# Decoder step on one core: expert rows gathered in the order they are stored and reordered by the PSUM copy, first up weights in eight halves, one combine earlier

## The chip, the cores and the metric

The kernel runs on one core of a Trainium2 chip. The metric is the device time of one execution in microseconds, as the median of several runs. The profile is of one execution; its span goes from the first to the last instruction.

## The reference

One layer of a decoder for 256 prompt tokens and 8 single-token sequences with 1024 cached positions each, D = 1024, everything float32:

```python
xn = rmsnorm(x, g_mix)
q, k, v, b_gate, c_gate, h_in = jnp.split(xn @ w_in, SPLIT_POINTS, axis=-1)
att = moba_attend(rope(q), k_all, v_all, pos)          # 8 heads of 64
conv_y = b_gate * short_conv(c_gate * h_in)            # 512 channels, 3 taps
hres = x + jnp.concatenate([att, conv_y], -1) @ w_out
hn = rmsnorm(hres, g_ffn)
# two-level router: one of 4 groups, then 2 of its 8 experts; gates sum over both
h = jax.nn.silu(hn @ w_gate[e]) * (hn @ w_up[e]) * gate[e]   # 32 experts, D -> 256
y = rmsnorm(hres + sum_e h @ w_down[e], g_final)
```

The expert weights are 32 times 1 MB each of gate, up and down, 96 MB in all. They and the 33.5 MB of the paged cache are most of what the core reads.

## The kernel before

**Stages.** The first stage (to about 203 us of the profile) projects, gathers cache pages by indirect DMA, attends, convolves, applies `w_out` and routes. It is cut into some 250 named steps (`steps["H10"]` and so on); the string `ORDER` (line 36) sets in which order they are recorded, and each engine executes its instructions in that order. The second stage is a loop over eight groups of four experts (line 1273).

**Tokens** stand in three tiles: tile 0 and 1 are the prompt, 128 rows each, tile 2 holds the 8 samples (`NR`). The residual rows are `yres[token, tile, 1024]`. A token's slot within an expert is its rank among the expert's tokens, 32 slots an expert; `rank` (`prk`) counts, `onehot` (`Pg`) turns ranks into a 0/1 matrix tokens x 128 slots for the group.

**One group.** `gather_mm` multiplies `Pg` with the rows (`px`, 128 slots x 512 columns, two halves `hf` of D); `gather_rows` copies `px` from PSUM to the row tile `xr`; `gather_T` transposes it (`pxt`) and scales it into `xg`; `mm_exp` multiplies with gate (`pgt`) and up weights (`pup`), four experts side by side in 32-column strips; SiLU times up gives `sh`, its transpose `hT`; `down` gives `pyy`; `gated` scales it by the routing weight into `Y` as a high and a low part; `combine_all` spreads `Y` back to tokens (`pz`) and adds it to `yres`. The combine of a group is recorded inside the next one, behind its gate product.

**Orders of columns.** The expert weights lie in memory so that partition p holds rows 8p to 8p + 7 of D: `w_gate.rearrange("o e (p c) f -> (o e) p (c f)", c=8)`. So `xg` needs, for each c, the elements D = 8p + c. For group 0 `gather_mm` reads `yres` as f32 with that order in the moving operand:

```python
rhs=yres[:, t, :].rearrange("t (p c) -> t c p", c=8)[:, 4 * hf:4 * hf + 4, :]
```

For the later groups the rows are split once into a high and a low part (`hn`, `hlo`; `norm2_hi` a cast on ACT, `norm2_lo` a difference on DVE), and these are stored in the order (c p), so that the products read neighbours. Tile 0 is split by the last step of `ORDER` (`hl0`), tile 1 in group 0 around the up product, tile 2 after it. The copies of `gather_rows` are plain.

**Weights and queues.** SP issues the loads, in the order of recording. Expert weights go through a ring of 15 buffers of 1 MB (`tags`, line 1149: two of tag c9, nine rk, four rw, which earlier held activations, cache rows and projection weights). The order is gate 0, down 0, the first two gates of group 1, then the up weights of group 0, then the rest. Up 0 has no place in the ring: `room1` and `room2` reserve six tiles of 512 KB (`uh`, from the pool c4 of ten) and four of 256 KB (`uq`, pool c2). The loads into them are recorded behind all steps (lines 1133 to 1137 and 1155 to 1165). The tiles `xh`, `xr`, `xg`, `hn`, `hlo` and `Y` come from the pool c4 as well, in turn.

**The last group** (`LAST` = 7) loads up in halves and down in three pieces; between its gate and up products stand the combine of group 6, maps and gates (`ppt`, `pgs`), three products that put `yres` into PSUM (`before`, `pzl`) and 12 dummy products (`keep_warm`, `warm`).

Of the kernel before, what the change touches and what calls it, by code (L numbers as in the profile page):

```python
# [19 lines left out]
D = 1024  # L20
# [21 lines left out]
cv2 b3 B10 b2 V3 cv0 V0 c2 c3 ov V2 V1 B13 eB1 G25 o010 kvs pe0 o000 eB3 G26 eB0 G27 G28 G29 o110 G30 V5 eB2 V4  # L42
o001 V6 H00 G31 o011 V7 H01 l00 pa pe o100 R0 l01 L0 ra0 rb0 rc0 o101 as co room1 rd0 re0 z0 z1 rk0 oh0 y0
y1 H10 H20 H21 l20 R2 l21 L2 ra2 rb2 room2 o111 rc2 rd2 l10 o112 H11 R1p H12a R1 H12b rk2 oh2 l11 l12 L1 ra1 rb1 rc1
g00 g01 rsa g20 rk1p rk1 oh1 g21 g10 ga0 g11 gt0 ga1 rsb gt1 rd1 sl re2 re1 hl0
"""
# [42 lines left out]
def hymba_step(ctx: ExitStack, tc: tile.TileContext, x_prompt, x_sample, cache_k, cache_v, state_conv,  # L89
# [22 lines left out]
    def c4(name, shape, dt=F32):  # L112
        return wp.tile(shape, dt, name=name, tag="c4", bufs=10)
# [11 lines left out]
    with tc.manual_schedule():  # L125
# [719 lines left out]
        def norm2_hi(t, a, w):  # L845
            n, p = NR[t], slice(a // 8, (a + w) // 8)
            if a == 0:
                hn[t] = c4(f"hn{t}", [128, 8, 128], F32R)
# [4 lines left out]
            S.copy(hn[t][:n, :, p].rearrange("t c p -> t p c"),  # L853
                   yres[:n, t, a:a + w].rearrange("t (p c) -> t p c", c=8))

# [7 lines left out]
        def norm2_lo(t, a, w):  # L863

            n, p = NR[t], slice(a // 8, (a + w) // 8)
            if t not in hlo:
                hlo[t] = c4(f"hlo{t}", [128, 8, 128], F32R)
            V.tensor_tensor(
                hlo[t][:n, :, p], yres[:n, t, a:a + w].rearrange("t (p c) -> t c p", c=8),
                hn[t][:n, :, p].bitcast(F32), op=OP.subtract)  # L870

# [155 lines left out]
        def gather_mm(grp, hf, tiles):  # L1027


            if (grp, hf) not in PX:  # L1030
                PX[grp, hf] = ps("px", "qb")
            first, last = (0, 2) if grp == 1 else (0, 1)
            for t in tiles:
                if grp == 0:
                    T.matmul(PX[grp, hf], lhsT=fl(PgS[grp], t, 128).bitcast(F32),
                             rhs=yres[:, t, :].rearrange("t (p c) -> t c p", c=8)[:, 4 * hf:4 * hf + 4, :],
                             start=t == first, stop=t == last)
                    continue
                n = 40 if t == 2 else 128
                lows = (0,) if t == 2 else (0, 1)  # L1040
                for low in lows:
                    T.matmul(PX[grp, hf], lhsT=fl(PgS[grp], t, n),  # L1042
                             rhs=(hn, hlo)[low][t][:n, 4 * hf:4 * hf + 4, :].rearrange("t c p -> t (c p)"),
                             start=t == first and low == 0, stop=t == last and low == lows[-1])

        XR = {}

        def gather_rows(grp, hf):
            if hf == 0:
                XR[grp] = c4("xr", [128, 8, 128])  # L1050
            rows_, px = XR[grp][:, 4 * hf:4 * hf + 4, :].rearrange("s c p -> s (c p)"), PX.pop((grp, hf))
            w = 256 if grp == 0 else 512
            S.copy(rows_[:, 0:w], px[:, 0:w])  # L1053
            if w < 512:
                V.tensor_copy(rows_[:, w:512], px[:, w:512])

# [63 lines left out]


        SPLIT = {}

        @step("room1")
        def _():
            for j in (0, 1, 3):
                SPLIT[0, "u", j] = [c4("uh", [128, 1024]) for _ in range(2)]

        @step("room2")
        def _():  # L1130
            SPLIT[0, "u", 2] = [c2("uq", [128, 512]) for _ in range(4)]

        def load_split(grp, nm, j, lst, view):
            ts = lst[grp, j] = SPLIT[grp, nm, j]
            w = 2048 // len(ts)
            for i, t in enumerate(ts):
                SP.dma_start(t, view[4 * grp + j][:, w * i:w * i + w])

        for name in ORDER.split():
            steps.pop(name)()  # L1140
        assert not steps, steps
# [12 lines left out]

        for grp in range(NE // 4):
            for lst, view, nm in ((gw, wg_v, "g"), (uw, wu_v, "u"), (dw, wd_v, "d")):
                for j in range(4):
                    if (grp, nm, j) == (1, "g", 2):
                        for k in (0, 1, 3, 2):
                            load_split(0, "u", k, uw, wu_v)  # L1160
                    if (grp, nm, j) in SPLIT:
                        continue
                    lst[grp, j] = ring(f"{nm}{grp}{j}", next(it))
                    if grp < LAST or nm == "g":
                        SP.dma_start(lst[grp, j], view[4 * grp + j])
        for a, b in ((0, 1024), (1024, 2048)):
# [106 lines left out]
        for grp in range(NE // 4):  # L1273
# [211 lines left out]
```

## Time and profile before

| | us |
|---|---|
| median of 3 runs (lowest to highest) | 429.58 (429.26 to 432.44) |
| profiled execution | 428.75 |
| its span | 426.7 |
| PE busy | 379.3 (89%) |
| DVE, ACT, POOL busy | 198.6, 94.0, 101.6 |
| moved by DMA | 155.05 MB, mean 363 GB/s |

The profile names groups by line, engine, operation and tile ("px<-yres,Pg" is written from those two). An f32 product leaves two records. "PEclk" is the share of TensorE's full clock that was granted. A wait "A <- B: 12.8, 1, 12.8" is total us, times, longest. SPq is SP's queue of DMA issues; a DMA row there has the time of its issue, not of its transfer.

### The profile page before, as it was taken

The numbers are of one execution on the slowest core, as the hardware profiler recorded it, in microseconds if no ns is written. First come the engines' busy times: TensorE is split into PE (matmuls) and PEld (weight loads), VectorE is DVE, ScalarE is ACT, GpSimd is POOL, SyncE is SP. The second block draws the span as 40 slices with busy tenths as digits, with TensorE's granted clock in tenths as the row PEclk, the third lists the DMA queues.
The fourth block names the chain that finished last, engine by engine and source line by source line (L and its number), as shares of the span: only waits on it lengthen the run. The fifth ranks groups of instructions, "written<-read, shape, count | busy, mean of one in ns | idle before, by whom it ended". The sixth has DMA issues, their size and how long they took to land.

```text
span 426.7 us, 6625 instructions
## 1 busy us (share of the span) xinstructions
PE 379.3 (89%) x2646; PEld 208.8 (49%) x2646; DVE 198.6 (47%) x389; ACT 94.0 (22%) x240; POOL 101.6 (24%) x99
## 2 busy tenths in 40 slices
PE   7999997999999999898999999996986987969971
PEld 6354354668775335363555455642533543524530
DVE  2257986899672014671763242430430431332045
ACT  4221314274330000311640111110020130110033
POOL 2727888978306000000200000000000000000031
PEclk9999999999999999988899899996996996997997
DMA  7999987879988999949899999999999999999903
GB/s 258 395 360 416 382 340 259 326 218 413 419 335 312 422 419 423 414 150 384 323 422 424 421 419 420 422 420 422 421 419 423 419 419 422 422 416 404 322 5 104
DMA packets 33125, 155.05 MB, mean 363 GB/s; under 512 B 3084, under 2 KB 5338, under 8 KB 18244
## 3 DMA queue, kind: packets, MB, share of 16 engines
q1 hardware_dynamic: 27472, 119.70, 70.3%
q0 software_dynamic: 5008, 33.80, 20.1%
q10 hardware_dynamic: 612, 1.11, 0.7%
q8 instruction: 22, 0.36, 0.3%
q14 instruction: 11, 0.09, 0.1%
HBM read 152.41 MB, written 2.20 MB: 362 GB/s over the span
## 4 chain that ended last, share of the span: by engine, by line
PE 58%; DMA 23%; DVE 9%; issue 4%; POOL 3%; ACT 1%; SPq 1%; DVEq 0%; ACTq 0%; POOLq 0%
DMA u<-in_w_up_dram 12%; DMA g<-in_w_gate_dram 9%; PE py L779 7%; PE pgt L1205 6%; PE pup L1205 5%; PE pyy L1219 4%; PE pz L1236 4%; PE px L1042 4%; PE pov L724 3%; PE acck L242 3%; PE accB L561 3%; DVE Sd L489 3%; PE accv L242 2%; PE accq L242 2%; DMA yres<-in_x_sample_dram 2%
## 5 line engine op out<-in xcount | busy, mean ns | idle before, releaser
L1205 PE MATMUL pgt<-g,xg 128*32 128x256 f32 x512 | 47.6, 481 | 18.0 <-DMA g<-in_w_gate_dram 17.7
L1270 DVE TENSOR_TENSOR yres<-yres,pz 128x512 f32<-128x512 f32 (+1 forms) x42 | 25.7, 672 | 53.6 <-PE pz L1236 53.6
L1176 POOL TENSOR_TENSOR PGw<-Pg,G 128x384 f32<-128x384 f32 x8 | 6.7, 843 | 171.6 <-PE pgs L1181 88.1
L1205 PEld LDWEIGHTS pgt<-g,xg 128*32 128x32 f32 x512 | 21.0, 137 | 45.7 <-DMA g<-in_w_gate_dram 24.0
L483 POOL TENSOR_TENSOR K<-K,qv 128x2048 f32<-128x2048 f32 x9 | 40.7, 4538 | 5.3 <-DMA K<-in_cache_k_dram,idx 3.1
L489 DVE TENSOR_REDUCE Sd<-K 128x32 f32<-128x2048 f32 x16 | 35.9, 2276 | 5.9 <-POOL K L483 5.9
L1219 PE MATMUL pyy<-d,hT 128*32 128x512 f32 (+1 forms) x272 | 32.1, 591 | 0.6 <-DVE hT L1318 0.6
L779 PE MATMUL py<-wo,mixT 128*128 128x512 f32 (+1 forms) x72 | 29.1, 552 | 0.0
L1205 PE MATMUL pup<-u,xg 128*32 128x256 f32 x448 | 25.6, 380 | 0.0
L1236 PE MATMUL pz<-Y,PT 128*128 128x512 f32 (+1 forms) x90 | 23.1, 405 | 0.0
L1228 DVE SCALAR_TENSOR_TENSOR Y<-pyy,gsl,Y 128x512 fp32r<-128x512 f32 (+1 forms) x17 | 12.1, 719 | 23.6 <-ACT Y L1227 23.6
L1296 DVE SCALAR_TENSOR_TENSOR sh<-pup,rsl,sh 128x256 f32<-128x256 f32 x8 | 5.4, 670 | 34.1 <-PE pup L1205 26.5
L1227 ACT ACTIVATE Y<-pyy,gsl 128x512 fp32r<-128x512 f32 (+1 forms) x17 | 11.2, 660 | 45.2 <-PE pyy L1219 45.1
L315 POOL DMA_INDIRECT V<-in_cache_v_dram,idx x16 | 15.6, 974 | 22.2 <-PE pov L724 18.2
L1053 ACT COPY xr<-px 128x512 f32<-128x512 f32 (+1 forms) x16 | 8.9, 559 | 50.7 <-PE px L1042 38.6
L779 PEld LDWEIGHTS py<-wo,mixT 128*128 128x128 f32 x72 | 13.2, 190 | 12.6 <-issue 12.1
L1042 PE MATMUL px<-hn,Pg 128*128 128x512 f32 (+1 forms) x42 | 19.2, 480 | 0.0
L315 POOL DMA_INDIRECT K<-in_cache_k_dram,idx x16 | 15.5, 971 | 14.7 <-DMA K<-in_cache_k_dram,idx 7.9
L1205 PEld LDWEIGHTS pup<-u,xg 128*32 128x32 f32 x448 | 13.8, 110 | 8.6
L1236 PEld LDWEIGHTS pz<-Y,PT 128*128 128x128 f32 (+1 forms) x90 | 13.2, 155 | 9.7 <-issue 2.9
L1219 PEld LDWEIGHTS pyy<-d,hT 128*32 128x32 f32 x272 | 8.8, 112 | 17.9 <-issue 16.0
L485 DVE TENSOR_TENSOR K<-K,qb 128x2048 f32<-128x2048 f32 x7 | 16.0, 2280 | 2.3 <-DMA K<-in_cache_k_dram,idx 2.3
(333 smaller groups left out, 607.1 us busy)
## 6 DMA issues: line engine op xcount, KB each, us to landing
g<-in_w_gate_dram SPq DMA_DIRECT2D x32, 1024.0 KB, 19.8
d<-in_w_down_dram SPq DMA_DIRECT2D x28, 1024.0 KB, 17.5
u<-in_w_up_dram SPq DMA_DIRECT2D x24, 1024.0 KB, 19.9
wo<-in_w_out_dram SPq DMA_DIRECT2D x4, 1024.0 KB, 16.9
u<-in_w_up_dram SPq DMA_DIRECT2D x8, 512.0 KB, 12.1
uh<-in_w_up_dram SPq DMA_DIRECT2D x6, 512.0 KB, 11.8
wk<-in_w_in_dram SPq DMA_DIRECT2D x2, 1024.0 KB, 14.4
wv<-in_w_in_dram SPq DMA_DIRECT2D x2, 1024.0 KB
```

The source lines that it names most:

```text
L242: T.matmul(acc, lhsT=xnT[:, cc, 128 * t:128 * t + 128], rhs=W[pn, kk][:, c, :], start=cc == 0, stop=cc == 7)
L315: P.indirect_dma_start(out=t, out_offset=None, in_=src, in_offset=bass.IndirectOffsetOnAxis(ap=idx[:, b, hh:hh + 1], axis=0))
L483: P.tensor_tensor(kslots[i], kslots[i], qv[:, None, :].to_broadcast([128, 4, 512]), op=OP.mult)
L485: V.tensor_tensor(kslots[i], kslots[i], qbs[b][:, None, :].to_broadcast([128, 4, 512]), op=OP.mult)
L489: V.tensor_reduce(Sd[:, b, 4 * hh:4 * hh + 4, :].rearrange("p i h -> p (i h)"), kslots[i].rearrange("p i (h d) -> p (i h) d", h=8), axis=A ...
L561: T.matmul(acc[:, 0:264], lhsT=W[pn, kk][:, c, 128 * m:128 * m + 128], rhs=xnT[:, cc, 0:264], start=cc == 0, stop=cc == 7)
L779: T.matmul(po[:, lo:lo + w], lhsT=mixT[:, c, 128 * t:128 * t + 128], rhs=wo[n, c // 4][:, c % 4, lo:lo + w], start=c == 0, stop=c == 7, sk ...
L1042: T.matmul(PX[grp, hf], lhsT=fl(PgS[grp], t, n), rhs=(hn, hlo)[low][t][:n, 4 * hf:4 * hf + 4, :].rearrange("t c p -> t (c p)"), start=t == ...
L1205: T.matmul(dst[32 * j:32 * j + 32, 0:256], lhsT=xg[:, c, 32 * j:32 * j + 32], rhs=w[:, 256 * k:256 * k + 256], start=c == 0, stop=c == 7, ...
L1219: T.matmul(py[32 * j:32 * j + 32, 0:w], lhsT=hT[:, c, 32 * j:32 * j + 32], rhs=dw[grp, j][:, 1024 * c + a:1024 * c + b], start=c == 0, sto ...
L1236: T.matmul(pz, lhsT=PTS[grp][:, 128 * t:128 * t + NR[t]], rhs=Y[:, i, 0:w], start=start and i == 0, stop=i == 1, skip_group_check=more)
L1270: V.tensor_tensor(yv, yv, pz[:m], op=OP.add)
```

## The change

**Rows in their own order.** `gather_mm` reads `yres`, and `hn` and `hlo`, as they stand: half hf is the columns 512 hf to 512 hf + 511, that is p from 64 hf, all c. The tiles `hn` and `hlo` become plain [128, 1024] copies. `gather_rows` now writes `xr` through a rearranged view (c is 128 elements apart), so a half fills a part of all eight c; every transpose needs both halves.

**Order of the first group.** In `ORDER`, `g20 g21` stand ahead of the rank of tile 1, and the sums `rsa` behind it; both copies `ga0 ga1` stand ahead of both transposes `gt0 gt1`. The step `hl0` is gone: tile 0 and tile 1 are split in group 0 behind the up product (`norm2_hi`) and behind the gates (`norm2_lo`).

**Up 0** is eight `uh` tiles of 512 KB from c4; `uq` and `room2` are gone. The loads are recorded inside the steps `ld0` and `room1`.

**The combine of group 6** is recorded at the end of group 6 instead of behind the gate product of group 7.

```diff
-o001 V6 H00 ... as co room1 rd0 re0 z0 z1 rk0 oh0 y0
-y1 H10 H20 H21 l20 R2 l21 L2 ra2 rb2 room2 o111 ...
-g00 g01 rsa g20 rk1p rk1 oh1 g21 g10 ga0 g11 gt0 ga1 rsb gt1 rd1 sl re2 re1 hl0
+o001 V6 H00 ... as co ld0 room1 rd0 re0 z0 z1 rk0 oh0 y0
+y1 H10 H20 H21 l20 R2 l21 L2 ra2 rb2 o111 ...
+g00 g01 g20 g21 rk1p rk1 oh1 rsa g10 ga0 g11 ga1 rsb gt0 gt1 rd1 sl re2 re1
...
-            S.copy(hn[t][:n, :, p].rearrange("t c p -> t p c"),
-                   yres[:n, t, a:a + w].rearrange("t (p c) -> t p c", c=8))
+            S.copy(hn[t][:n, a:a + w], yres[:n, t, a:a + w])
...
-            V.tensor_tensor(
-                hlo[t][:n, :, p], yres[:n, t, a:a + w].rearrange("t (p c) -> t c p", c=8),
-                hn[t][:n, :, p].bitcast(F32), op=OP.subtract)
+            V.tensor_tensor(hlo[t][:n, a:a + w], yres[:n, t, a:a + w], hn[t][:n, a:a + w].bitcast(F32), op=OP.subtract)
...
-                             rhs=yres[:, t, :].rearrange("t (p c) -> t c p", c=8)[:, 4 * hf:4 * hf + 4, :],
+                             rhs=yres[:, t, 512 * hf:512 * hf + 512],
...
-                             rhs=(hn, hlo)[low][t][:n, 4 * hf:4 * hf + 4, :].rearrange("t c p -> t (c p)"),
+                             rhs=(hn, hlo)[low][t][:n, 512 * hf:512 * hf + 512],
...
-            rows_, px = XR[grp][:, 4 * hf:4 * hf + 4, :].rearrange("s c p -> s (c p)"), PX.pop((grp, hf))
-            w = 256 if grp == 0 else 512
+            rows_ = XR[grp][:, :, 64 * hf:64 * hf + 64].rearrange("s c p -> s p c")
+            px = PX.pop((grp, hf)).rearrange("s (p c) -> s p c", c=8)
+            w = 32 if grp == 0 else 64
             S.copy(rows_[:, 0:w], px[:, 0:w])
-            if w < 512:
-                V.tensor_copy(rows_[:, w:512], px[:, w:512])
+            if w < 64:
+                V.tensor_copy(rows_[:, w:64], px[:, w:64])
...
+        @step("ld0")
+        def _():
+            load(0, "g", range(4))
+            load(0, "d", range(4))
+            load(1, "g", (0, 1))
+
+        @step("room1")
+        def _():
+
+            for j in range(4):
+                uw[0, j] = [c4("uh", [128, 1024]) for _ in range(2)]
+                for i, t in enumerate(uw[0, j]):
+                    SP.dma_start(t, wu_v[j][:, 1024 * i:1024 * i + 1024])
...
-                combine_all(grp - 1, Ys)
+                if grp < LAST:
+                    combine_all(grp - 1, Ys)
                 slot_maps(grp)
                 slot_gates(grp)
-            else:
-                norm2_hi(1, 0, 512)
-                norm2_hi(1, 512, 512)
...
             if grp == 0:
                 slot_maps(grp)
+                for t in (0, 1):
+                    for a in (0, 512):
+                        norm2_hi(t, a, 512)
...
                 slot_gates(grp)
-                norm2_lo(1, 0, 512)
-                norm2_lo(1, 512, 512)
+                for t in (0, 1):
+                    for a in (0, 512):
+                        norm2_lo(t, a, 512)
                 norm2_both(2)
...
+            if grp == LAST - 1:
+                combine_all(grp, Ys)
```

**What moves on PE ahead of the first gate product.** `px` is the gather product, `prk` the rank of tile 1, `prs` the norm factor of each slot, `pxt` the transposes. Before:

```order
191 L1035 MATMUL px<-yres,Pg 128x512 x2
192 L1066 MATMUL prs<-rsb_1112,Pg 128x1
193 L1066 MATMUL prs<-rsb_1251,Pg 128x1
194 L1035 MATMUL px<-yres,Pg 128x512
195 L1001 LDWEIGHTS onesb__72
196 L1001 MATMUL prk<-A,onesb__72 128x32
197 L1001 LDWEIGHTS onesb__72
198 L1001 MATMUL prk<-A,onesb__72 128x32
199 L1008 LDWEIGHTS trib
200 L1008 MATMUL prk<-A,trib 128x32
201 L1035 MATMUL px<-yres,Pg 128x512 x3
202 L1076 MATMUL pxt<-ident,xr 128x128 x4
```

After:

```order
191 L1031 MATMUL px<-yres,Pg 128x512 x4
192 L997 LDWEIGHTS onesb__72
193 L997 MATMUL prk<-A,onesb__72 128x32
194 L997 LDWEIGHTS onesb__72
195 L997 MATMUL prk<-A,onesb__72 128x32
196 L1004 LDWEIGHTS trib
197 L1004 MATMUL prk<-A,trib 128x32
198 L1064 MATMUL prs<-rsb_1112,Pg 128x1
199 L1064 MATMUL prs<-rsb_1281,Pg 128x1
200 L1031 MATMUL px<-yres,Pg 128x512 x2
201 L1064 MATMUL prs<-rsb_1336,Pg 128x1
202 L1074 MATMUL pxt<-ident,xr 128x128 x8
```

Four of the six `px` stand ahead of the rank instead of three, two behind it, and the eight transposes come in one row.

**What SP's loads of up 0 wait for** (DMAHW names a lane of earlier transfers, the other names an engine that read or wrote the buffer). Before:

```order
33 L1137 DMA uh<-in_w_up_dram 128x1024 [waits DVE_49,DMAHW0_49,PE_49,Activation_49]
34 L1137 DMA uh<-in_w_up_dram 128x1024 [waits DMAHW1_49,PE_49]
35 L1137 DMA uh<-in_w_up_dram 128x1024 [waits DVE_49,DMAHW2_49,PE_49,Activation_49]
36 L1137 DMA uh<-in_w_up_dram 128x1024 [waits DMAHW3_49,DVE_49,PE_49]
37 L1137 DMA uq<-in_w_up_dram 128x512 [waits DMAHW4_49]
```

After:

```order
33 L1148 DMA uh<-in_w_up_dram 128x1024 [waits DMAHW0_49]
34 L1148 DMA uh<-in_w_up_dram 128x1024 [waits DMAHW1_49,Activation_49]
35 L1148 DMA uh<-in_w_up_dram 128x1024 [waits DMAHW2_49]
36 L1148 DMA uh<-in_w_up_dram 128x1024 [waits DMAHW3_49]
37 L1148 DMA uh<-in_w_up_dram 128x1024 [waits DMAHW4_49,DVE_49]
38 L1148 DMA uh<-in_w_up_dram 128x1024 [waits DMAHW5_49,DVE_49]
39 L1134 DMA g_1430<-in_w_gate_dram 128x2048 [waits DMAHW6_49,PE_49]
```

No `uh` waits for PE any more; the engine waits that are left are for the attention's tiles (lines 521, 534, 544 and 708). The gates of group 1 wait for PE, which reads `w_out` out of the same buffers.

**PE at the end of group 6.** Before, behind the gate product of group 7:

```order
944 L1205 MATMUL pgt<-g_1586,xg 32x256
945 L1236 MATMUL pz<-Y,PT 128x512 x2
946 L1236 MATMUL pz<-Y,PT 8x512 x2
947 L1236 MATMUL pz<-Y,PT 128x512 x4
950 L1192 MATMUL ppt<-ident,Pg 128x128 x2
```

After:

```order
894 L1219 MATMUL pyy<-d_1568,hT 32x512
895 L1236 MATMUL pz<-Y,PT 128x512 x2
896 L1236 MATMUL pz<-Y,PT 8x512 x2
897 L1236 MATMUL pz<-Y,PT 128x512 x4
900 L1205 MATMUL pgt<-g_1570,xg 32x256
```

The combine `pz` stood between `pgt` and `ppt` and now stands between group 6's `pyy` and `pgt`.

More of the change, by code (lines that the diff above doesn't have):

```diff
@@ L42 @@
 cv2 b3 B10 b2 V3 cv0 V0 c2 c3 ov V2 V1 B13 eB1 G25 o010 kvs pe0 o000 eB3 G26 eB0 G27 G28 G29 o110 G30 V5 eB2 V4
[L43 to L45 removed]
+o001 V6 H00 G31 o011 V7 H01 l00 pa pe o100 R0 l01 L0 ra0 rb0 rc0 o101 as co ld0 room1 rd0 re0 z0 z1 rk0 oh0 y0
+y1 H10 H20 H21 l20 R2 l21 L2 ra2 rb2 o111 rc2 rd2 l10 o112 H11 R1p H12a R1 H12b rk2 oh2 l11 l12 L1 ra1 rb1 rc1
+g00 g01 g20 g21 rk1p rk1 oh1 rsa g10 ga0 g11 ga1 rsb gt0 gt1 rd1 sl re2 re1
 """
@@ L845, in norm2_hi @@
         def norm2_hi(t, a, w):
-            n, p = NR[t], slice(a // 8, (a + w) // 8)
+            n = NR[t]
             if a == 0:
-                hn[t] = c4(f"hn{t}", [128, 8, 128], F32R)
+                hn[t] = c4(f"hn{t}", [128, D], F32R)
                 if t == 2:
@@ L863, in norm2_lo @@
         def norm2_lo(t, a, w):
-            n, p = NR[t], slice(a // 8, (a + w) // 8)
+            n = NR[t]
             if t not in hlo:
-                hlo[t] = c4(f"hlo{t}", [128, 8, 128], F32R)
-            V.tensor_tensor(
-                hlo[t][:n, :, p], yres[:n, t, a:a + w].rearrange("t (p c) -> t c p", c=8),
-                hn[t][:n, :, p].bitcast(F32), op=OP.subtract)
+                hlo[t] = c4(f"hlo{t}", [128, D], F32R)
+            V.tensor_tensor(hlo[t][:n, a:a + w], yres[:n, t, a:a + w], hn[t][:n, a:a + w].bitcast(F32), op=OP.subtract)
         def norm2_log(t, k):
@@ L1119, in hymba_step @@
         steps["rsb"] = lambda: gather_rs(0, (1,))
[L1122 to L1141, printed above, removed]
         wg_v = w_gate.rearrange("o e (p c) f -> (o e) p (c f)", c=8)
@@ L1153, in ring, with load @@
             return c9(name, (128, 2048)) if tag == "c9" else slot(name, tag)
[L1155 to L1165, printed above, removed]
+        def load(grp, nm, js):
+            lst, view = {"g": (gw, wg_v), "u": (uw, wu_v), "d": (dw, wd_v)}[nm]
+            for j in js:
+                lst[grp, j] = ring(f"{nm}{grp}{j}", next(it))
+                SP.dma_start(lst[grp, j], view[4 * grp + j])
+        @step("ld0")
[9 more added lines that the diff above has]
+                    SP.dma_start(t, wu_v[j][:, 1024 * i:1024 * i + 1024])
+        for name in ORDER.split():
+            steps.pop(name)()
+        assert not steps, steps
+        load(1, "g", (2, 3))
+        load(1, "u", range(4))
+        load(1, "d", range(4))
+        for grp in range(2, LAST):
+            for nm in "gud":
+                load(grp, nm, range(4))
+        load(LAST, "g", range(4))
+        for j in range(4):
+            uw[LAST, j] = ring(f"u{LAST}{j}", next(it))
+        for j in range(4):
+            dw[LAST, j] = ring(f"d{LAST}{j}", next(it))
         for a, b in ((0, 1024), (1024, 2048)):
@@ L1394, in hymba_step @@
             n = NR[t]
-            hs = c4("hs", [128, 8, 128])
+            hs = c4("hs", [128, D])
             V.tensor_tensor(hs[:n], hn[t][:n].bitcast(F32), hlo[t][:n].bitcast(F32), op=OP.add)
@@ L1401, in hymba_step @@
                 for c in range(4):
-                    T.transpose(pv_[:, c, 0:n], hs[:n, 4 * hf + c, :], ident[:n, :n])
+                    T.transpose(pv_[:, c, 0:n], hs.rearrange("t (p c) -> t c p", c=8)[:n, 4 * hf + c, :], ident[:n, :n])
                 V.tensor_tensor(hnT2[:, 4 * hf:4 * hf + 4, 128 * t:128 * t + n], pv_[:, :, 0:n],
```

1 line of the change is left out of this document (removed).

## Prediction

> **What bounds the kernel now.** I read the page first: PE is busy for 89% of the span and the DMA engines move 420 GB/s in most of the second half, so I need to know which of the two sets the end in which stage. I cut the span into stretches around the one place where the page's DMA row falls (columns: stretch in us, length, busy us of PE, PEld, DVE, ACT, POOL with instruction counts, granted PE clock, DMA share, GB/s):
>
> ```profile
> 161.00:183.60 22.60, 20.63 (x158) 11.70 (x154) 13.85 (x61) 4.27 (x13) 1.13 (x2) 1.00 1.00 412
> 183.60:188.90 5.30, 4.78 (x24) 3.41 (x25) 4.25 (x23) 1.30 (x7) 0.61 (x2) 1.00 0.08 26
> 188.90:194.00 5.10, 5.10 (x9) 2.06 (x8) 1.81 (x9) 0.00 (x0) 0.00 (x0) 0.51 0.85 214
> 194.00:207.00 13.00, 11.66 (x64) 4.66 (x66) 4.96 (x27) 4.39 (x13) 0.00 (x0) 0.80 1.02 423
> 207.00:209.60 2.60, 2.60 (x56) 1.44 (x48) 2.37 (x4) 2.40 (x4) 0.32 (x1) 1.00 0.44 110
> 209.60:300.00 90.40, 83.44 (x797) 45.20 (x789) 33.66 (x52) 17.68 (x36) 4.82 (x6) 0.94 1.01 418
> ```
>
> DMA stands still from 183.6 to 188.9, runs at half rate to 194, and runs dry again at 207 to 209.6. After that it is full to the end of the weights. So from 209.6 on the end is a fixed distance behind: the bytes left by a constant rate, and then a tail. Whatever starts that stream earlier moves the end by as much. The waits of SP, 180 to 212 us, say what holds it:
>
> ```profile
> SPq L1165 <- PE pgt L1205: 12.8, 1, 12.8
> SPq L1137 <- DVE xh L842: 6.0, 1, 6.0
> ```
>
> The 6 us wait is a half of up weights (uh) whose buffer was free late: the first hole. The 12.8 us wait is the ring of 15 weight buffers, full until the first group's gate product (pgt) gives its four back: the second hole. Of the two, only the second decides. At 183.6 six and a half MB of loads were left that may run before pgt ends (one uh, the four uq, two g, three u); without any hole they would be done at 183.6 + 6.5 x 2.5 = about 200 (1 MB is 1.049 MB / 418 GB/s = 2.5 us), and then DMA waits for pgt anyway. So the time of pgt's end, 208.3, is the number to move; filling the first hole only takes care that 200 comes before it.
>
> PE on the way there:
>
> ```profile
> 187.67 3.89 PE L1035 MATMUL px<-yres,Pg 128*128 128x512 f32 x4
> 191.38 0.91 PE L1066 MATMUL prs<-rsb,Pg 128*128 128x1 f32 x4
> 192.22 2.18 PE L1035 MATMUL px<-yres,Pg 128*128 128x512 f32 x2
> 194.22 0.34 PE L1001 MATMUL prk<-A,onesb__72 128*128 128x32 bf16 x2
> 194.54 5.84 PE L1035 MATMUL px<-yres,Pg 128*128 128x512 f32 x6
> 200.20 0.62 PE L1076 MATMUL pxt<-ident,xr 128*128 128x128 f32 x4
> 203.34 4.97 PE L1205 MATMUL pgt<-g,xg 128*32 128x256 f32 x64
> ```
>
> The six products px (two records each) take 11.9 us of it. The tail, from the chain of waits:
>
> ```profile
> 385.03 6.26 PE pgt L1205 x58
> 391.29 3.00 PE pz L1236 x12
> 401.89 3.63 PE pup L1205 x64
> ```
>
> When the last gate weights land at 385.0, everything is PE's chain to the end, and 3.0 us of it is the combine (pz) of the group before.
>
> **The change, part by part.**
>
> Part 1, px read in its own order. Rates of the same 128x512 f32 product:
>
> ```profile
> L1035 PE MATMUL px<-yres,Pg 128*128 128x512 f32 x12 | 11.9, 1128 | 0.0
> L242 PE MATMUL acck<-wk,xnT 128*128 128x512 f32 x32 | 14.5, 596 | 0.0
> L1247 PE MATMUL pzl<-yres,ident 128*128 128x512 f32 x4 | 2.0, 618 | 0.0
> ```
>
> px reads every eighth element of yres: 11.9 / 12 = 0.99 us a record. Reads of neighbours take 14.5 / 32 = 0.45 (acck) and 2.0 / 4 = 0.50 (pzl, which reads yres itself). So one px falls from 1.98 to 0.9 us, at full clock. The clock:
>
> ```profile
> 189.00:195.80 6.80, 6.80 (x14) 2.87 (x13) 2.19 (x11) 0.00 (x0) 0.00 (x0) 0.50 0.91 265
> 195.80:202.60 6.80, 5.48 (x13) 1.72 (x12) 1.21 (x3) 1.32 (x5) 0.00 (x0) 1.00 1.03 434
> 202.60:206.00 3.40, 3.38 (x31) 1.55 (x34) 2.41 (x18) 2.08 (x6) 0.00 (x0) 0.50 1.01 424
> ```
>
> The strided px cost the same in the half-clock stretch and in the full one, so they were bound by their read; the new ones will feel the clock. Half clock comes in stretches of 3.4 or 6.8 us. What decided the one at 189.0 lies before it and is mostly unchanged, so I keep it, and let it end after 3.4 us since the products are dense now. The four px that stand ahead of the rank (two tiles, two halves) start at 187.7 as before: 1.3 us at full speed, then half until 192.4, then the rest: 1.3 / 0.9 = 1.4 products, 3.4 / 1.8 = 1.9, 0.7 x 0.9 = 0.6 us: done at 193.0. From there to the third tile's one-hot took
>
> ```profile
> 194.97 0.29 DVE L1023 TENSOR_TENSOR Pg<-rka,tab 128x128 fp32r<-128x128 f32 x1
> ```
>
> 195.3 - 194.2 = 1.1 us: 194.1. The last two px, 1.8: 195.9.
>
> Part 2, the order moves into the PSUM copy. It writes the row tile with a stride, and the first transposes need both halves of it. The nearest rows:
>
> ```profile
> L853 ACT CAST hn<-yres 128x512 fp32r<-128x512 f32 x4 | 4.2, 1146 | 0.0
> L461 ACT CAST qhi<-partq x1: 618/618/618, 21.8 to 21.8; 128x512 fp32r<-128x512 f32 x1
> L1053 ACT COPY xr<-px 128x512 f32<-128x512 f32 x14 | 8.2, 585 | 38.6 <-PE px L1042 38.6
> L1055 DVE COPY xr<-px 128x256 f32<-128x256 f32 x2 | 0.8, 425 | 4.7 <-ACT xr L1053 4.7
> L462 DVE TENSOR_TENSOR qlo<-partq,qhi x1: 692/692/692, 22.5 to 22.5; 128x512 fp32r<-128x512 f32 x1
> ```
>
> The old hn cast wrote exactly the new pattern: 1.15 against 0.62 without stride. So a strided xr copy costs between 0.59 (no penalty) and 1.15; I take 1.15, and for the quarter-size ones of the first group ACT 0.65 and then DVE 0.65 (half of the penalty on each). In the first group: 195.9 + 1.3 = 197.2, eight transposes in a row instead of four, 1.15 us (four take 0.62 in the rows above): 198.3, pgt at its old 4.97: ends at 203.3. Old end 208.3. **Term 1: 5.0 us.** Bounds: with no half clock ahead of the rank (191.3 instead of 193.0) and a dense pgt (3.6 us, its later groups) it ends near 200, a gain of 8.3; with half clock to 195.8 near 204.5, a gain of 3.8. In the other groups the copy hides: the second copy (1.15) runs under prs and pht, the products that PE has between px and the transposes (0.9 + 0.3 us). Without that cover it is 0.6 us a group on PE, where DMA, not PE, is late.
>
> Part 3, hi and lo split of tile 0 moves into the first group, all contiguous. Six casts at 0.62 = 3.7 us on ACT, six differences at 0.69 = 4.1 on DVE, where tile 1 and 2 alone took
>
> ```profile
> 213.48 2.14 DVE L868 TENSOR_TENSOR hlo<-yres,hn 128x512 fp32r<-128x512 f32 x2
> 215.65 2.12 DVE L868 TENSOR_TENSOR hn<-yres,hn 8x512 fp32r<-8x512 f32 x2
> 213.68 3.64 PE L1219 MATMUL pyy<-d,hT 128*32 128x512 f32 x32
> ```
>
> 4.3 us. DVE is no later than before; behind it wait the scaled outputs Y and px of group 1, as now. Cover: pyy, 3.6 us of PE. What comes late if I am wrong is the release of group 1's gate buffers. After pgt the queue gets 4 MB = 10 us of work, the next buffers come with pyy, 217.3 - 208.3 = 9.0 us later, so about 1 us may be lost here before DMA runs dry. Cost taken: 0, at most 1.5.
>
> Part 4, uh issued early. In the order, the new uh wait for old transfers and for long finished reads of attention tiles; no xh or rs row of the second norm stands among the releasers. So DMA has no hole before 200. The four 256 KB pieces, during which DMA moved 214 GB/s, are gone too. Worth by itself: nothing, as 200 is already ahead of pgt's end. It is what lets term 1 count in full: with the old waits the loads would still end near 207, and at least 3.7 of the 5 us would be lost.
>
> Part 5, the combine of group 6 ahead of the last pgt. It runs while PE waits for g:
>
> ```profile
> 378.33 0.59 PE L1205 MATMUL pgt<-g,xg 128*32 128x256 f32 x2
> ```
>
> ```profile
> 383.50:390.40 6.90, 5.37 (x52) 2.56 (x56) 0.00 (x0) 0.00 (x0) 0.00 (x0) 0.51 1.02 409
> 404.00:406.00 2.00, 1.48 (x28) 0.65 (x20) 0.38 (x1) 0.00 (x0) 0.00 (x0) 1.00 0.31 104
> ```
>
> pgt's first two records stand at 378.3, right behind pyy, and the rest waits for 385.0. pz (3.0) put there, with its Y coming some 0.7 late, is through by 382. **Term 2: 3.0 us**, if what follows does not wait for weights instead. pup would start at 398.9. The last u half is issued at 385.0 and landed 10 us after its issue:
>
> ```profile
> L1168 SPq DMA_DIRECT2D u<-in_w_up_dram x8: 327/328/328, 367.5 to 385.0; - x8
> DMA to landing us min/median/max: 10.2/12.1/14.0
> ```
>
> 395.2, so it is there. The last d piece streams until about 405 and its products start at 411.6 then. Nothing new waits. **Term 3:** pgt's 58 records take 6.26 at half clock and 58 / 64 x 3.6 = 3.3 at full. With pz in the gap the idle stretch shrinks from 6.6 to about 3.3 us, so half clock should be shorter, but I doubt that it goes: 1.0 us of the possible 3.0.
>
> [...]
>
> Sum: 5.0 + 3.0 + 1.0 = 9.0 us off the profiled execution (426.7 span, 428.75 in all, 0.8 under the median): 429.6 - 9.0 = **420.6 us**.
>
> **The rivals.**
>
> (a) Forecast, chance 0.54: 420.6, with its own range 418 to 423.
>
> (b) The clock goes along: no half clock ahead of the rank or in pgt 0 (8.3), and a warm last pgt (3 + 3). Up to 14.3; with two thirds of the further 5.3 us it is 417.0. For it: dense products where strided ones stood, work in the gap. Against: the clock also fell at 202.6 with PE busy. 0.24.
>
> (c) px is no faster (its time is f32, not stride), and the copies are slower: 7.9 + 1.1 + 3.9 + 1.3 + 1.15 + 5.0 from 187.7 ends pgt at 208.0; only the tail counts, 4.3: 425.3. Against: pzl reads the same yres at half the time. 0.08.
>
> (d) The tail waits for weights after all, so that terms 2 and 3 go: 424.6. Against: 395.2 and 405 above. 0.06.
>
> (e) Part 3 holds group 1 back and DMA runs dry for 2 us: 422.6. 0.06.
>
> (f) Slower: the strided copy from PSUM costs far more than from SBUF. From one pgt to the next PE needs 245.7 - 222.6 = 23.1 us where it does not wait for weights:
>
> ```profile
> 222.64 3.66 PE L1205 MATMUL pgt<-g,xg 128*32 128x256 f32 x64 [0.35 <-DVE xg L1078]
> 245.73 3.63 PE L1205 MATMUL pgt<-g,xg 128*32 128x256 f32 x64
> ```
>
> DMA needs 12 x 2.5 = 30 us a group. Two copies a group would decide from 0.6 + 3.5 = 4 us each on; at 5.2 each a group is 32.2, six groups lose 13 against the 9: about 433. The nearest row says 1.15. 0.02.
>
> **How the numbers follow.** Of all cases (a), (b), (d), (e) and half of (c) lie under 425.3, 1% off: faster 0.91, within 1% 0.07, slower 0.02; 1% is about what a measurement of this kernel can tell from no change. The range 416.5 to 425.0 leaves out the far end of (b), most of (c) and (f).
>
> **What would show it.** px records of the first group near 0.45 to 0.9 us instead of 0.99; pgt 0 ending 16 us after px starts instead of 20.6; DMA full from 161 to about 200, one hole until pgt's end, none later; strided xr copies near 1.15; pz of group 6 before the last g lands and pup 8 us after pgt instead of 10.6. Wrong would be: a DMA hole inside groups 0 to 3, pup waiting for u, or px still at 0.99.

## The result

The changed kernel takes 416.64 us (median of 4 runs, 415.40 to 417.39); the kernel before, beside it, 431.01 (429.26 to 433.26). The ratio is 0.966, with an interval of 0.960 to 0.972: faster by 14.4 us, where 9.0 were forecast. As a ratio on the 429.58 of the forecast it is 415.0 us, below the range. The profiled executions stand 13.3 us apart (spans 426.7 and 413.5), and it can be said where each of these lies. All rows here are from the two profiles:

| piece, from one row of PE to another | before, us | after, us | gained |
|---|---|---|---|
| start to first px of group 0 | 187.67 | 187.59 | 0.1 |
| first px to end of group 0's gate product | 20.64 | 12.67 | 8.0 |
| from there to the last gate weights | 176.72 | 176.81 | -0.1 |
| last gate weights to start of pup | 16.79 | 10.68 | 6.1 |
| pup to the last product | 15.52 | 15.58 | -0.1 |
| last product to the end | 9.38 | 10.14 | -0.8 |

So two stages moved, the two that were forecast, and each by more than forecast: 8.0 instead of 5.0, and 6.1 instead of 4.0.

**The first stage after.** PE in order of time (start, length, instructions and count):

```profile
187.59 3.68 PE L1031 MATMUL px<-yres,Pg 128*128 128x512 f32 x8
...
191.38 0.67 PE L1064 MATMUL prs<-rsb,Pg 128*128 128x1 f32 x4
192.14 1.98 PE L1031 MATMUL px<-yres,Pg 128*128 128x512 f32 x4
...
195.43 1.09 PE L1074 MATMUL pxt<-ident,xr 128*128 128x128 f32 x8 [1.19 <-DVE xr L1053]
196.60 3.66 PE L1205 MATMUL pgt<-g,xg 128*32 128x256 f32 x64
```

Eight records of px in 3.68 us: 0.46 each, where 0.99 stood before. And the gate product takes 3.66, not 4.97: it has the full clock. The stretches (columns as in the prediction: busy us of PE, PEld, DVE, ACT, POOL, then granted clock, DMA share, GB/s):

```profile
183.60:188.90 5.30, 4.78 (x25) 3.51 (x26) 4.27 (x23) 1.30 (x7) 0.61 (x2) 1.00 1.03 420
188.90:194.00 5.10, 5.01 (x19) 2.46 (x17) 2.29 (x12) 0.60 (x1) 0.00 (x0) 1.00 1.01 422
194.00:200.00 6.00, 4.73 (x75) 3.12 (x77) 4.67 (x24) 3.49 (x11) 0.00 (x0) 1.00 0.96 399
200.00:202.40 2.40, 2.40 (x52) 1.43 (x44) 0.71 (x3) 0.47 (x1) 1.28 (x2) 1.00 0.52 130
202.40:300.00 97.60, 89.13 (x860) 49.41 (x852) 36.07 (x60) 21.37 (x40) 4.79 (x6) 0.97 1.01 421
```

The granted clock is 1.00 up to 202.4 and 0.97 behind it; before it was 0.51 in the second stretch. DMA has one short hole, at 200 to 202.4, and is full from there.

**The tail after**, from the chain of waits and from PE's order of time:

```profile
357.07 19.96 DMA g<-in_w_gate_dram
377.07 3.64 PE pgt L1205 x58
```

```profile
370.90 3.62 PE L1236 MATMUL pz<-Y,PT 128*128 128x512 f32 x12
374.46 0.74 PE L1205 MATMUL pgt<-g,xg 128*32 128x256 f32 x6
...
387.75 3.66 PE L1205 MATMUL pup<-u,xg 128*32 128x256 f32 x64
```

The combine (pz) stands ahead of the last weights, and the 58 records of the gate product take 3.64 instead of 6.26 us.

### The profile page after: what moved, and what is told of

It reads as the page before. It is cut to its first block, busy times and chain, and to the rows that moved or that the text cites. A ratio compares the mean times of both kernels' runs of the same rounds, so it can differ in the third digit from the quotient of the medians.

```text
span 413.5 us, 6611 instructions
## 1 busy us (share of the span) xinstructions
PE 368.2 (89%) x2646; PEld 206.2 (50%) x2646; DVE 195.3 (47%) x389; ACT 96.9 (23%) x240; POOL 101.3 (25%) x99
## 5 line engine op out<-in xcount | busy, mean ns | idle before, releaser
L1205 PE MATMUL pgt<-g,xg 128*32 128x256 f32 x512 | 43.2, 456 | 15.6 <-DMA g<-in_w_gate_dram 15.2
L1205 PEld LDWEIGHTS pgt<-g,xg 128*32 128x32 f32 x512 | 20.1, 130 | 39.4 <-DMA g<-in_w_gate_dram 20.2
L1219 PE MATMUL pyy<-d,hT 128*32 128x512 f32 (+1 forms) x272 | 31.2, 571 | 0.6 <-DVE hT L1319 0.6
L1051 ACT COPY xr<-px 128x512 f32<-128x512 f32 (+1 forms) x16 | 15.7, 983 | 43.1 <-PE px L1038 36.0
L779 PEld LDWEIGHTS py<-wo,mixT 128*128 128x128 f32 x72 | 13.2, 190 | 12.6 <-issue 12.1
## 6 DMA issues: line engine op xcount, KB each, us to landing
d<-in_w_down_dram SPq DMA_DIRECT2D x28, 1024.0 KB, 18.1
```

The costliest lines, as they stand in the source:

```text
L779: T.matmul(po[:, lo:lo + w], lhsT=mixT[:, c, 128 * t:128 * t + 128], rhs=wo[n, c // 4][:, c % 4, lo:lo + w], start=c == 0, stop=c == 7, sk ...
L1205: T.matmul(dst[32 * j:32 * j + 32, 0:256], lhsT=xg[:, c, 32 * j:32 * j + 32], rhs=w[:, 256 * k:256 * k + 256], start=c == 0, stop=c == 7, ...
L1219: T.matmul(py[32 * j:32 * j + 32, 0:w], lhsT=hT[:, c, 32 * j:32 * j + 32], rhs=dw[grp, j][:, 1024 * c + a:1024 * c + b], start=c == 0, sto ...
```

## The experiments

Twelve runs. All but two are the changed kernel with something undone or added; these two are the changed kernel itself, as a yardstick on the same chip. Columns streamed, below, is my count from the trace's records: each record's columns (512 for px, 1 for prs), times the share of its time that lies in the window, times its tile's share of 128x128 (a quarter on a 128x32 tile). A window is one of the stretches of 3.41 us at whose ends alone the granted clock changes in the traces, up to the last products (in the profile before, for example, at 188.98, 195.81, 202.63 and 206.05).

### px with its stride again

```diff
-                             rhs=yres[:, t, 512 * hf:512 * hf + 512],
+                             rhs=yres[:, t, :].rearrange("t (p c) -> t c p", c=8)[:, 4 * hf:4 * hf + 4, :],
```

(and plain copies to xr in group 0)

> The changed kernel with one part undone: the products px of group 0 read every eighth element of yres again, and their copies to xr are plain. Everything else as changed. Theory (the rate of px sets the end of the first gate product, and its slow reading is also what took the clock away): px back to 0.99 us a record; the clock goes to half near 189 again; the first gate product ends at 206.7 to 208.5 instead of 200.2; DMA is through with its loads near 200 and stands for 6 to 8 us; the profiled time is 421.5 to 423.5 against 415.4. Rival (the early up weights made the gain by filling the hole at 183.6 to 188.9): DMA is full there in this kernel too, so the time stays under 418.

422.02 us (420.06 to 424.74), ratio to before 0.978 (0.973 to 0.983): 5 us of the gain are gone though the weights came as early as in the changed kernel. PE and DMA in its profile:

```profile
191.89 7.58 PE L1031 MATMUL px<-yres,Pg 128*128 128x512 f32 x8
...
200.33 3.92 PE L1031 MATMUL px<-yres,Pg 128*128 128x512 f32 x4
...
206.21 3.77 PE L1210 MATMUL pgt<-g,xg 128*32 128x256 f32 x64
```

```profile
183.60:200.00 16.40, 15.88 (x48) 9.03 (x47) 6.82 (x35) 1.30 (x7) 0.61 (x2) 0.72 0.98 407
200.00:211.50 11.50, 11.41 (x112) 5.95 (x116) 5.38 (x27) 4.32 (x13) 1.02 (x1) 0.85 0.03 8
```

px is back at 0.95 to 0.98 a record, and the section from px to the gate product's end takes 18.1 us against 12.7. DMA stands still for 11 us: early loads without an early gate product only lengthen the wait of the ring (19.5 us for pgt here, 12.8 before). The rival (the loads alone made the gain) falls: DMA moves 407 GB/s from 183.6 to 200 here, and the median is 422.0. One thing was not expected: px starts 4.3 us late, at 191.89. That is followed up below.

### The up weights late again, and then the hole again

Late alone: uh in six halves and uq in four quarters at the old place, all else as changed.

```diff
+            for j in (0, 1, 3):
+                SPLIT[0, "u", j] = [c4("uh", [128, 1024]) for _ in range(2)]
...
+            SPLIT[0, "u", 2] = [c2("uq", [128, 512]) for _ in range(4)]
```

> The changed kernel with the other part undone: the first group's up weights in six halves and four quarters at their old place behind the second norm's buffers, gate and down loads recorded as before. Dense px, the copies and the moved combine stay. Theory (DMA time lost ahead of the full stream is what counts, so both parts are needed): hole of 5 to 6 us from 183.6 again and half rate for 5 us behind it, no hole at the end of the first gate product, since the loads run late to 206 or 207; of the 8.0 us 5.5 to 7 are lost: 421 to 422.5 profiled. Rival (only the end of the first gate product counts, filling the first hole is worth nothing): it still ends near 200, so 415.4 to 417.

417.76 us (416.76 to 420.42): 1.1 us over the 416.64 of the changed kernel, as a ratio to before 0.971 (0.965 to 0.977) against 0.966, so not clear of the noise, and not the 5.5 to 7 expected. But the profile shows that the run did not bring the hole back:

```profile
183.60:188.90 5.30, 5.01 (x24) 4.25 (x23) 2.69 (x14) 0.98 (x6) 0.00 (x0) 0.77 1.04 402
```

So the experiment says nothing on the hole's price; it says that the place of the loads did not make it. In its trace no load of up 0 waits for an engine by more than 0.4 us at a time, where the kernel before had 6.0 for xh. And the last gate weights land at 379.72, which is the changed kernel's 377.07 but for px, which starts 2.75 us later here. What still differed from the kernel before was hl0, the split of tile 0, which took two of the ten buffers at the end of the first stage and so, it seems, moved which old tile each uh lands on. The next run puts it back:

```diff
-g00 g01 g20 g21 rk1p rk1 oh1 rsa g10 ga0 g11 ga1 rsb gt0 gt1 rd1 sl re2 re1
+g00 g01 g20 g21 rk1p rk1 oh1 rsa g10 ga0 g11 ga1 rsb gt0 gt1 rd1 sl re2 re1 hl0
```

> The changed kernel with the late up weights of the run before and with the split of tile 0 (hl0) back at the end of the first stage: the buffers of the two tiles hn and hlo of tile 0 are handed out there again, and the up halves wait for the second norm as in the kernel before. Dense px, copies and the moved combine stay. Theory (the DMA time lost ahead of the full stream counts, and it was the place of hl0, not the place of the loads, that made the hole): DMA hole of 5 to 6 us from 183.6, half rate behind it, loads through only near 207, first gate product done 12.7 us after px starts, near 200; the stream starts full at 206 to 207 instead of 202: 4 to 6 us above the changed kernel, 421 to 423. Rival (the hole is worth nothing when px is dense): 416.5 to 417.5.

424.11 us (422.04 to 426.79), ratio to before 0.983 (0.978 to 0.989), with 417.08 for the changed kernel on the same chip: 7.0 us lost, where 4 to 6 were expected. Waits of SP, then the stretches:

```profile
SPq L1135 <- PE pgt L1214: 11.1, 2, 5.8
SPq L1152 <- DVE xh L842: 7.0, 1, 7.0
```

```profile
183.60:188.90 5.30, 4.78 (x33) 4.14 (x32) 4.04 (x20) 1.30 (x7) 0.64 (x2) 1.00 0.08 32
188.90:194.00 5.10, 5.01 (x18) 2.53 (x18) 3.10 (x15) 0.00 (x0) 0.00 (x0) 1.00 0.65 163
194.00:207.00 13.00, 11.38 (x156) 6.98 (x159) 8.71 (x31) 7.07 (x20) 2.65 (x3) 1.00 1.02 416
```

The gate product of group 0 ends as early as in the changed kernel, 12.66 us after px starts, and yet the last gate weights land at 384.51 against 377.07. DMA lost its time at 183.6 to 194 and has none to make good behind it. The two are tied. Dense px with the hole bring the last gate weights 0.5 us forward (384.51 against 385.03 before; 1.6 if px's start, 1.1 late here, is allowed for); no hole with strided px 2.7 (386.56 in the first run, less the 4.3 by which px started late there); both together 8.0.

### The combine back behind the last gate product, without and with filler

```diff
-                if grp < LAST:
-                    combine_all(grp - 1, Ys)
+                combine_all(grp - 1, Ys)
...
-                combine_all(grp, Ys)
```

> The changed kernel with the combine of group 6 back behind the last gate product. Theory: the twelve pz (3.0 us) are on the chain again, and the idle gap without them takes the clock from the last gate product (6.3 instead of 3.6 us): 5.2 to 5.8 us, 420.5 to 421.2 profiled. Rival (the clock of the last gate product is a matter of where the gap falls in the clock's windows, not of pz): 3.0 only, 418.4.

420.22 us (419.98 to 422.15). The last weights land at 378.46 and pup starts at 394.16: 15.7 us, against 10.68 in the changed kernel. The gate product takes 5.18 us there, where 6.3 were expected: the clock was lost for one window of 3.4 us, not two.

```profile
378.46 5.18 PE L1205 MATMUL pgt<-g,xg 128*32 128x256 f32 x58 [1.88 <-DMA g<-in_w_gate_dram]
```

The second kernel has the same order, with 26 filler products at the end of group 6, where the changed kernel has its combine:

```diff
             if grp == LAST - 1:
-                combine_all(grp, Ys)
+                keep_warm(26)
```

> As the run with the combine put back, but 26 products of 128 columns that nobody reads stand in its place behind the down product of group 6. Theory (the clock follows what PE streams in a window of 3.41 us): the last gate product stays at 3.6 us, only the 3.0 us of pz come back: 418.0 to 419.0 profiled. Rival (the clock comes from elsewhere): gate product 6.3 us as with the combine put back, 420.5 to 421.2.

418.63 us (418.33 to 419.16), as the theory had it. Its PE, in order of time:

```profile
372.09 6.07 PE L298 MATMUL warm<-ident 128*128 128x128 f32 x52
378.09 3.69 PE L1205 MATMUL pgt<-g,xg 128*32 128x256 f32 x64
381.71 3.07 PE L1236 MATMUL pz<-Y,PT 128*128 128x512 f32 x12
...
392.32 3.66 PE L1205 MATMUL pup<-u,xg 128*32 128x256 f32 x64
```

Same order, clock kept. The filler ends as the last weights land (issued at 358.2, 19.9 us to landing), so that it is 14.23 us from there to pup, 1.5 less, and 2.6 less than before (16.79), where the clock was lost for two windows. The 3.55 that remain to the changed kernel's 10.68 are pz itself (3.0) and 0.55 of wait for PT, which is ready by itself when pz is out of the way.

### Busy, but streaming nothing

```diff
+                T.matmul(w[:, 0:1], lhsT=ident, rhs=ident[:, 0:1], start=True, stop=True)
...
-g00 g01 g20 g21
+one g00 g01 g20 g21
```

> The changed kernel with ten products of one column each, which nobody reads, between the last router product and px of group 0. They keep PE busy for about 1.4 us but stream almost nothing. Theory (the clock follows the columns streamed in a window of 3.41 us, not the time that PE is busy): the window up to about 188.7 falls from 2096 to some 800 columns, half clock from there on, and dense px take 0.9 us a record in it; the first gate product ends 1.4 us later by the ten products and 2 to 4 us later by the clock, 203.5 to 205.5; the profiled time is 3 to 5.5 over 415.4. Rival (only a window in which PE idles takes the clock): full clock, the gate product ends near 201.6, the profiled time is 1 to 1.5 over 415.4.

425.42 us (one run). Two things make the sum larger than expected: an f32 product is two records, so that ten products took 3.33 us and not 1.4; and px would have started late here too, near 192. What the run was for is in three windows of the clock, and in px:

```profile
189.62:193.03 3.41, 2.89 (x25) 2.50 (x23) 2.66 (x13) 0.51 (x2) 0.61 (x2) 1.00 1.01 423
193.03:196.44 3.41, 3.41 (x14) 2.89 (x15) 1.96 (x10) 0.00 (x0) 0.00 (x0) 0.50 1.02 423
196.44:199.86 3.42, 3.42 (x6) 1.35 (x5) 0.00 (x0) 0.00 (x0) 0.00 (x0) 0.50 0.90 376
```

```profile
195.32 5.93 PE L1037 MATMUL px<-yres,Pg 128*128 128x512 f32 x8
...
202.12 1.98 PE L1037 MATMUL px<-yres,Pg 128*128 128x512 f32 x4
```

The first window has PE busy for 2.89 of 3.41 us, just as the window 185.31 to 188.72 of the changed kernel, which kept its clock (both windows are shown further down); it streams 963 columns where that one streams 2,096, and the clock goes. In the second PE is busy all the time, with 550 columns, and the clock stays at half. The third has 2,081 and gets it back. So in this run the clock does not go by idle time alone. Dense px at half clock then cost what the prediction had reckoned: eight records 5.93 us, and px to gate product 14.92 instead of 12.67.

### Different amounts of filler in the waits of groups 4 to 6

```diff
-            mm_exp(pgt, gw, grp)
+            mm_exp(pgt, gw, grp, {4: {1: 11}, 5: {2: 7}, 6: {2: 9}}.get(grp, {}))
```

(n products behind the first record of weight tile j)

> The changed kernel with products of 128 columns, which nobody reads, put among the first products of the gate product while it waits for its weights: 11 in group 4, 7 in group 5, 9 in group 6. Without them the window ahead of each of these gate products has 130 to 260 columns and the gate product runs at half clock (5.9 to 6.6 us). Theory (a threshold between about 1370 and 1620 columns in a window): group 4, near 1650 columns, full clock and 3.7 us; group 5, near 1100, half clock and 6 us or more; group 6, near 1400, on the edge. The time stays within 0.5 us of 415.4, since DMA sets the pace there. Rival (any work in the gap keeps the clock): all three at full clock. Rival (none does): all three at half.

415.07 us (one run). All three gate products ran at full clock (58 records in 3.64 us), so the ladder does not find the threshold that was expected: each product is two records, all three fills were twice what I had meant, and the "any work" rival stands as far as this run goes. For a threshold there are only the windows themselves. Over fourteen profiles, of the windows at full clock with fewer than 900 columns 54 lost the clock and 1 kept it; with 900 to 1,500, 20 and 16; with 1,500 to 2,000, 4 and 42; above 2,000, 10 and more than 1,300. Of those at half clock, none of the 85 with 1,500 or more stayed there, and 34 of the 37 below did. So the clock goes with the count in most windows and not in all. Seven of the ten odd ones stand at one place, the px and prs of group 1, and I have no reason for them.

### Filler before the last gate product

```diff
-            mm_exp(pgt, gw, grp)
+            mm_exp(pgt, gw, grp, {LAST: {2: 12}}.get(grp, {}))
```

> The changed kernel with 12 products of 128 columns, which nobody reads, in the gap of the last gate product, before its last weights land. Theory (in the profiled run the window there had 1555 columns, close to the threshold, so that some runs lose the clock and 2.6 us; the granted clock of the runs was 0.956 to 0.968): with 1536 columns more it never does; the median falls by 0.5 to 1.5 us to 415 to 416, and the runs lie closer together. Rival (it never lost it): 416.6 as the changed kernel.

> The changed kernel itself, beside the one with the filled gap: 416.6 median and 415.4 to 417.4 as first measured.

416.28 us (414.54 to 417.82, 6 runs) against 417.15 (415.00 to 418.47, 6 runs): no difference that this shows, and the spread stayed. The reason I gave for the spread was not its main one: the profile of the changed kernel taken beside it has the last gate product at 3.64 us without filler. It lost its time elsewhere:

```profile
175.39:178.80 3.41, 2.31 (x33) 1.12 (x25) 2.58 (x10) 1.93 (x5) 0.00 (x0) 1.00 1.02 417
178.80:182.21 3.41, 2.56 (x22) 2.28 (x23) 1.92 (x10) 0.72 (x2) 0.54 (x1) 0.50 1.02 410
182.21:185.63 3.42, 3.42 (x12) 2.85 (x10) 1.53 (x7) 0.00 (x0) 0.00 (x0) 0.50 1.02 411
```

In the wait for the second norm (near 178) the window has 1,094 columns, the clock falls for two windows, and px starts at 190.16 instead of 187.59. The profiles of before and after happen to be two in which it did not; of the ten others without filler at that place it fell in all, and px started at 188.7 to 192.0 (in the kernel with one-column products, these started at 192.0, and px behind them).

### Filler in the wait of the second norm, and less of it in the tail

```diff
-y1 H10 H20 H21
+y1 H10 kw H20 H21
...
+        steps["kw"] = lambda: keep_warm(6, "qb")
```

> The changed kernel with six products of 128 columns (two records each), which nobody reads, in PE's wait of 1.7 us for the second norm (177.9 to 179.6). Theory (in most runs the window of the clock that holds this wait has 460 to 1100 columns, the clock falls near 179 for one or two windows, and px starts at 188.9 to 190.2 instead of 187.6; the profile of the changed kernel happens to be one in which it does not): px always starts at 187.6 and the median falls by 1 to 2 us to 415.0 to 416.0, with a spread under 1.5 us instead of 3.5. Rival (the spread has another cause): median 416.6 to 417.2 and the same spread.

> The changed kernel itself, beside the filled ones: 416.6 to 417.2 median, 415 to 418.5 over all runs; px starts at 187.6 in few of its profiles.

415.19 us (413.79 to 415.93, 6 runs) against 417.08 (415.36 to 418.42, 6 runs); ratios to before 0.962 (0.958 to 0.965) and 0.966 (0.963 to 0.970). The theory holds for the median: the window at the wait now has 2,114 columns and the clock stays, px starts at 187.47.

```profile
176.16:179.57 3.41, 2.81 (x30) 2.38 (x31) 3.12 (x11) 2.21 (x7) 0.00 (x0) 1.00 1.01 408
179.57:182.99 3.42, 3.42 (x35) 3.07 (x35) 2.09 (x12) 0.00 (x0) 0.54 (x1) 1.00 1.04 414
```

The spread is 2.1 us, not under 1.5: in this profile the last gate product is one that lost a window (5.3 us), as in the changed kernel's own profile taken beside it. The second kernel also cuts the filler ahead of the last pup:

```diff
-KEEP = 12
+KEEP = 6
```

> As the run with the filled wait of the second norm, and the 12 products that keep the clock ahead of the last up product cut to 6 (1.45 us less). The last half of the up weights lands near 388.4 in the profile of the changed kernel, and its first record on PE comes half way through pup. Theory: pup starts 1.4 us earlier, its second half waits a little for its weights, 0.7 to 1.4 us gained: 414 to 415. Rival (the weights decide): pup ends no earlier, no gain, or a loss if the clock falls.

414.25 us (413.04 to 414.63, 6 runs), ratio to before 0.960 (0.957 to 0.964): the lowest median here, though its interval overlaps that of the kernel with 12 (0.958 to 0.965). pup starts at 386.23, 1.5 us earlier than in the changed kernel, and does not wait. The down product behind it does, for its own weights: 3.33 us instead of 2.77, so that pup to the last product takes 16.29 instead of 15.58 and half of the 1.5 us is lost again.

```profile
386.23 3.66 PE L1206 MATMUL pup<-u,xg 128*32 128x256 f32 x64
...
391.83 3.33 PE L1220 MATMUL pyy<-d,hT 128*32 128x512 f32 x24 [0.58 <-DVE hT L1320]
```

## Why the prediction was wrong in size, and where it was right

**Term 1 (5.0 forecast, 8.0 measured).** The bound and the chain hold: the last gate weights came 8.0 us earlier because the first gate product ended 8.0 earlier, at 200.26; the upper bound of the term (8.3, ending near 200) is what happened. px at 0.46 to 0.50, the first stage's copies at 0.59 for 0.65 forecast, transposes 1.09 for 1.15: each within 0.06. The step that failed is "What decided the one at 189.0 lies before it and is mostly unchanged, so I keep it". The window that decided is 185.57 to 188.98, and 1.3 us of px lie in it. Before:

```profile
185.57:188.98 3.41, 2.89 (x16) 1.80 (x15) 2.86 (x14) 0.85 (x4) 0.61 (x2) 1.00 0.04 8
188.98:192.39 3.41, 3.41 (x8) 1.60 (x7) 1.73 (x9) 0.00 (x0) 0.00 (x0) 0.50 0.82 202
```

After:

```profile
185.31:188.72 3.41, 2.89 (x18) 2.05 (x17) 2.75 (x13) 1.04 (x6) 0.61 (x2) 1.00 1.04 424
188.72:192.13 3.41, 3.33 (x13) 1.57 (x12) 2.36 (x12) 0.00 (x0) 0.00 (x0) 1.00 1.01 424
```

PE is busy for 2.89 us in both, and only the first loses the clock. Strided, they stream 0.5 columns a ns (512 in 0.99 us) and the window comes to 1,366 columns; dense, 1.1 a ns (512 in 0.46 us), and it comes to 2,096. The slow reading was itself what took the clock away: with the stride alone put back, the window that holds the start of px (189.42 to 192.83 in that run, PE busy for 2.89 us again) lost it too. In the eleven profiles with dense px (the one with one-column products apart), px to the end of the gate product takes 12.66 to 12.67 us at full clock wherever the windows fall; in the two with strided px the clock was lost there in both, twice each. So the 3.0 us that were missing are 1.7 in px and 1.3 in the gate product, as the working for the bound had them. My evidence against rival (b), "the clock also fell at 202.6 with PE busy", was the best evidence for it: that window, 199.22 to 202.63, holds strided px and a wait, 1,366 columns.

In the traces, every half-clock stretch up to the last products is one to three whole windows of 3.41 us (before, two from 188.98 and one from 202.63; in the strided run three, from about 179.2 to 189.4). Their grid stands between 4.4 and 7.3 us after the first instruction, from run to run (4.40 in the profile of the changed kernel, 4.66 before, 7.33 in the run with the filled last gate product). The clock was lost after busy windows too: a window of the strided run with PE idle for only 0.09 of 3.41 us lost it.

```profile
199.66:203.07 3.41, 3.32 (x8) 1.20 (x8) 0.70 (x3) 0.37 (x1) 0.00 (x0) 1.00 0.05 22
203.07:206.48 3.41, 3.41 (x16) 2.32 (x18) 1.22 (x4) 0.99 (x4) 0.00 (x0) 0.50 0.00 0
```

**Part 2** was right: the strided copies take 1.04 us (1.15 taken, 0.59 without stride) and hide: DMA is full at 421 GB/s from 202.4 to 300. **Part 3** was right in its cost: the gate product of group 1 starts 14.7 us behind the end of that of group 0, 14.3 before, and DMA does not run dry between them.

**Part 4** was right that term 1 counts in full only without the hole (7.0 us are lost with it; at least 3.7 forecast). Its reason, the early issue of uh, is not shown to be the one: late loads alone cost 1.1 us by the medians, within the noise, and brought no hole; late loads with hl0 in the first stage brought it. So leaving hl0 out of the first stage, an edit of part 3, was enough to close it. Whether the early issue would have been enough too, with hl0 at its old place, was not run.

**Term 2 (3.0 forecast, 3.5 measured)**: pz and half a microsecond of wait for PT, which I had not counted. **Term 3 (1.0 forecast)**: 2.6 in the profiled run, the whole of what could be had, since the 58 records take 3.64 us at full clock and not the 3.3 that the prediction had worked out. Before, the clock fell there though no wait of PE between two records was longer than 1.89 us. That half clock gets shorter with the idle stretch, from which the 1.0 came, was an estimate that no run shows: with the combine put back, and a longest wait of 1.88 us, the 58 records take 5.18 us and not 6.26.

In the changed kernel the clock is not kept safely there either. Of the ten profiles with the combine moved and nothing put into that wait, six show the last gate product at 3.64 us and four at 5.3; the difference goes with where the windows fall in that run. By the count of columns, the windows that hold the wait kept the clock with 909 to 1,555 columns and lost it with 819, 858, 899 and, against the order, 1,473.

**The finish** took 0.8 us more, which no term had. It takes 8.6 us in some profiles and 9.4 to 10.3 in others, across kernels; what sets that stays open.

So rival (b), with a chance of 0.24, was the case, and right in its mechanism: the clock went along in both places. Its full gain of 14.3 us came (14.1 in the two stages, 13.3 between the profiles with the longer finish, 14.4 by the medians), not the 12.6 that made its 417.0. That 417.0 stands near the measured 416.64 is luck: the kernel before took 431.01 beside it, 1.4 us more than the 429.58 that the forecast started from, and on that base the changed kernel comes to 415.0. The other rivals fell: px is faster (c), the tail does not wait for weights (d), DMA does not run dry behind group 0 (e), the copies cost 1.04 and not 4 (f).

## What to carry to other kernels

Before you keep a half-clock stretch in a sum, count the columns that PE streams in the 3.41 us ahead of it: here an operand read with a stride (1,366 columns, 2,096 when dense, PE busy for 2.89 us in both) and one-column products (550, PE busy throughout) lowered that count while PE looked busy, a wait lowered it too (1,094), and the edit that made px dense brought the clock back with it. A wait after which the clock fell in some runs and not in others made the runs of one kernel differ (profiled runs of 415.4 and 417.8 us); a few products that nobody reads, put into that wait, took 1.9 us off the median. And where a pool hands out buffers in turn, a hole may come from a step that only shifts the turn: undo each edit by itself, and both together, before you say which one closed it.

## What the runs showed of the hardware that was not expected

- A window in which PE was busy for all of its 3.41 us, most of it with one-column records, streamed 550 columns and left the clock at half. Of the full-clock windows in fourteen profiles, 54 of the 55 under 900 columns lost the clock, 20 of the 36 with 900 to 1,500, and 4 of the 46 with 1,500 to 2,000.
- The clock's grid shifts from run to run: in the three profiles of the changed kernel its windows start 4.40, 4.72 and 6.35 us after the first instruction (and every 3.41 us from there). The changed kernel took 415.0 to 418.5 us over sixteen runs; of its three profiles, the one that kept the clock in the wait for the second norm took 415.4 us, the two that lost it 417.8 and 418.0 (the last of them lost it at the last gate product too). With that wait filled, 2.1 us are left between the best and the worst of six.
